# The second layer's mixer modulation computed inside the first layer's output projection instead of inside its GLA mixer

## The chip, the cores and the metric

The kernel is one inference step on one Trainium2 chip. It runs on one core. The metric is device time in microseconds (us) of one execution.

## What is computed

Two layers, each on 576 rows of width 1024 (512 prompt rows and 8 sequences of 8 sampled rows):

```
for l in range(DEPTH):
    mod = silu(c) @ w_ada[l] + b_ada[l]
    sh1, sc1, g1, sh2, sc2, g2 = split(mod, 6)
    h = x * (1.0 + sc1) + sh1
    mix, st = mixer(h, ...)
    x = layer_norm(ALPHA * x + g1 * mix)
    h = x * (1.0 + sc2) + sh2
    x = layer_norm(ALPHA * x + g2 * hier_moe(h, l, p))
```

The mixer projects `h` with `w_in` (1024 x 3096), runs three head groups (GLA linear attention, retention, Mamba-2 SSD), joins them and multiplies by `w_out` (1024 x 1024). `hier_moe` is a mixture of 16 experts. The modulation `mod` depends only on `c`, which is known from the start: nine rows (one prompt, eight samples) times `w_ada[l]`, 1024 x 6144, 24 MB in float32 for each layer. So it may be worked out at any time before it is used.

## The kernel before

**The modulation in groups and steps.** `ada_steps(l, g)` is a generator that works out a third of a layer's modulation: group 0 is sh1 and sc1, group 1 is g1 and sh2, group 2 is sc2 and g2. It has eight steps. A step loads 128 rows by 2048 columns of `w_ada` (1 MB, line 263) into a buffer `wada` and issues four matmuls of 32 x 512 (line 266), which add into one PSUM tile `ada`; the trace shows each as two rows, so a step is 8 rows there. After the eighth step comes a tail: line 269 adds the bias on DVE, which frees `ada`, and then for group 0 four transposes (line 300) and copies into `modT`, for group 1 a store to DRAM (line 272), for group 2 more work on DVE, four small loads and transposes (lines 279 to 292).

```
        for k in range(KD):
            w = wraw.tile([128, 2048], F32, name="wada", tag="raw")
            sp.dma_start(w, a["w_ada"][l, 128 * k:128 * (k + 1), c0:c0 + 2048])
            for q in range(4):
                ...
                pe.matmul(acc[32 * q:32 * q + 32, :], sc_[:, k, :], w[:, o:o + 512], start=(k == 0), stop=(k == KD - 1))
            yield
```

The buffer pool `wraw` has three buffers of 1 MB, and they are handed out in program order to everything that streams weights: `wada`, the pieces of `w_in` (line 382), the four pieces of `w_out` (line 1535), the first expert's weights (line 1288). All these loads are issued by SP's queue, in order: a load that waits for its buffer holds up what stands behind it.

**The stages of a layer.** `phase_a` runs SSD and then GLA, each woven with a piece of the input projection (lines 403 to 405) and, through `weave`, with modulation steps at a rate given by a table. The GLA mixer goes tile by tile (lines 808 to 965): its chain passes from PE through ACT, DVE and POOL and back. `phase_b` does the output projection in two passes over five row tiles (tile 4, of 64 rows, first). Pass 1 takes the SSD half of `w_out` (`load_out(2)`, `load_out(3)`), while the retention heads `ret` run beside it, two advances a tile; pass 2 takes `load_out(0)` and `load_out(1)`, the GLA and retention half, and after each tile a layer norm, the routing of tokens and the stores to `hbuf`. Each `w_out` piece is split into a high and a low part, in halves, by ACT (line 335) and DVE (line 336). A tile of a pass is 24 matmuls of 128 x 512 (lines 1564 to 1566), and its result is taken from PSUM by DVE (line 1576, `mix`, two a tile). `phase_b` also takes a generator `fill`: it is advanced three times after each tile of pass 1 and twice after each tile of pass 2. Then `experts` runs the mixture.

**Where the groups stand.** Group (0, 0) is computed at the start. A table says where the others go, as (layer, group): `MODS_SSD[l]` beside layer l's SSD, `MODS_GLA[l]` beside its GLA, `MODS_B[l]` in its output projection as `fill`. Before the change (1, 0) and (1, 1) stand in layer 0's GLA, and (1, 2) in layer 1's output projection. The program is scheduled when it is built: each engine gets one fixed order, and waits there in order.

Of the kernel before, what the change touches and what calls it, by code (L numbers as in the profile page):

```python
# [52 lines left out]
RORDER = (0, 4, 1, 2, 3)  # L53

MODS_SSD = (((0, 1), (0, 2),), ())
MODS_GLA = (((1, 0), (1, 1),), ())
MODS_B = ((), ((1, 2),))
MODS_RATE = ((1.5, 0.0), (1.7, 0.0))

C_GQ, C_GK, C_GV, C_GA, C_GR = 0, 128, 256, 512, 528  # L60
# [101 lines left out]
def _body(nc, tc, a, ctx, dbg):  # L162
# [1303 lines left out]
    def chain(*gens):  # L1466
        for g in gens:
            yield from g

    def phase_a(l, S, hT, gates, sL, z):  # L1470

        norms = []
        mods = [chain(*[ada_steps(*g) for g in w[l]]) for w in (MODS_SSD, MODS_GLA)]
        with ExitStack() as st:
# [721 lines left out]
    for l in range(L):  # L2196
        with ExitStack() as sL:
# [13 lines left out]
            with ExitStack() as rst:  # L2211
                fill = chain(*[ada_steps(*g) for g in MODS_B[l]])
                last, finish = phase_b(l, gates, nrm, gst, slots, rqk, rv, x, R, tabs, rst, fill)
# [123 lines left out]
```

## Time and profile before

| | |
|---|---|
| time, median of 3 runs | 1433.18 us (1431.92 to 1436.41) |
| the profiled execution, its own time | 1432.89 us |
| its span | 1431.1 us |
| PE busy | 1239.5 us, 87% of the span |
| weight loads of PE (PEld) busy | 940.2 us, 66% |
| DVE busy | 832.9 us, 58% |
| ACT, POOL busy | 487.9 us and 478.3 us |
| moved by DMA | 267.24 MB, mean 187 GB/s |

The span is the time from the first to the last instruction of the profiled execution. Busy shares are averages over stages that are bound by different things; a change in one stage is judged from that stage. The two layers run the same code, so a stage of layer 0 can be laid beside the same stage of layer 1, which differs in the modulation steps woven into it.

### The profile page before, as it was taken

Reading aid. Unit: us, or ns where it says so; the run is one execution under the profiler, and the core shown is the slowest. Engines: PE = TensorE matmul, PEld = TensorE weight load, DVE = VectorE, ACT = ScalarE, POOL = GpSimd, SP = SyncE. Lnnn points to the kernel's source line nnn. Section 1 sums busy time; section 2 is a strip of 40 time slices with the busy share of each in tenths; the row PEclk is TensorE's granted clock in tenths of the full one; section 3 lists DMA queues with packets and bytes.
Section 4 is the critical chain, followed back from the end, with each engine's and each line's share of the span. In section 5 each row is a group of like instructions: output and inputs, shape, how many; then the busy total and the mean of one; then the engine's idle time right before and its main releaser. Section 6 shows DMA issues by size and latency. Waiting matters only on the chain. (4 is left out here: it accounts for less than half of the span.)

```text
span 1431.1 us, 21969 instructions
## 1 busy us (share of the span) xinstructions
PE 1239.5 (87%) x8166; PEld 940.2 (66%) x8166; DVE 832.9 (58%) x1911; ACT 487.9 (34%) x902; POOL 478.3 (33%) x388
## 2 busy tenths in 40 slices
PE   4999999998986688989899998999998668998893
PEld 1998677775865356666479887877576446666661
DVE  0577457346889433446777647545598951324548
ACT  0552133331344213444355223333034431333422
POOL 0014112125244455541242312133413453534315
PEclk7899999999987699989999998999998779999997
DMA  9545665865162577987524410015555254887642
GB/s 317 177 148 167 224 231 190 303 217 178 38 195 101 173 283 283 395 306 237 177 89 148 120 60 30 23 41 193 196 183 183 99 201 199 320 319 261 214 142 107
DMA packets 100606, 267.24 MB, mean 187 GB/s; under 512 B 30871, under 2 KB 59449, under 8 KB 81528
## 3 DMA queue, kind: packets, MB, share of 16 engines
q1 hardware_dynamic: 84600, 246.62, 49.2%
q0 software_dynamic: 15872, 18.89, 4.0%
q8 instruction: 77, 1.26, 0.4%
q14 instruction: 57, 0.47, 0.1%
HBM read 246.84 MB, written 47.63 MB: 206 GB/s over the span
## 5 line engine op out<-in xcount | busy, mean ns | idle before, releaser
L403 PE MATMUL ps<-whi,hT 128*128 128x256 f32 (+1 forms) x640 | 188.4, 294 | 1.6 <-DVE yi L721 0.8
L405 PE MATMUL ps<-whi,hT 128*128 128x256 f32 (+1 forms) x640 | 182.9, 286 | 2.0 <-DVE rq L360 1.9
L404 PE MATMUL ps<-wlo,hT 128*128 128x256 f32 (+1 forms) x640 | 182.9, 286 | 1.1 <-DVE wlo L330 1.1
L403 PEld LDWEIGHTS ps<-whi,hT 128*128 128x128 f32 (+1 forms) x640 | 117.6, 184 | 14.7 <-issue 10.3
L404 PEld LDWEIGHTS ps<-wlo,hT 128*128 128x128 f32 (+1 forms) x640 | 117.4, 183 | 3.8 <-issue 2.1
L405 PEld LDWEIGHTS ps<-whi,hT 128*128 128x128 f32 (+1 forms) x640 | 117.2, 183 | 3.5 <-DVE rq L360 2.1
L1386 POOL DMA_INDIRECT ybuf<-ys,srci x36 | 46.9, 1302 | 132.5 <-issue 52.6
L330 DVE TENSOR_TENSOR wlo<-wraw,whi 128x2048 fp32r<-128x2048 f32 x30 | 68.6, 2287 | 34.5 <-ACT whi L329 34.1
L393 PE MATMUL ps<-hT,whi 128*128 128x288 f32 x512 | 88.5, 294 | 0.0
L330 DVE TENSOR_TENSOR wlo<-w3rd,whi 128x2048 fp32r<-128x2048 f32 x22 | 67.7, 3078 | 24.3 <-ACT whi L329 23.1
L1355 PE MATMUL ps<-whi,xh 128*128 128x256 f32 x384 | 59.8, 301 | 22.8 <-ACT xh L1342 12.7
L393 PEld LDWEIGHTS ps<-hT,whi 128*128 128x128 f32 x512 | 74.6, 188 | 0.4 <-ACT zdt L532 0.4
L1564 PE MATMUL ps<-whi,mh 128*128 128x512 f32 (+1 forms) x160 | 70.2, 439 | 3.7 <-ACT mh L1550 3.7
L266 PE MATMUL ada<-wada,scond 128*32 128x512 f32 x384 | 57.1, 667 | 17.4 <-DMA wada<-w_ada 17.4
L1566 PE MATMUL ps<-whi,ml 128*128 128x512 f32 (+1 forms) x160 | 68.2, 431 | 3.3 <-DVE ml L1551 3.3
L1355 PEld LDWEIGHTS ps<-whi,xh 128*128 128x128 f32 x384 | 52.5, 203 | 26.7 <-ACT xh L1342 13.6
L1565 PE MATMUL ps<-wlo,mh 128*128 128x512 f32 (+1 forms) x160 | 69.5, 434 | 0.0
L1355 PE MATMUL ps<-wlo,xh 128*128 128x256 f32 x384 | 59.8, 303 | 9.5 <-DVE wlo L330 9.4
L843 POOL TENSOR_TENSOR qh<-qx,ex 128x256 f32<-128x256 f32 x32 | 31.3, 1008 | 99.5 <-issue 82.1
L1355 PEld LDWEIGHTS ps<-wlo,xh 128*128 128x128 f32 x384 | 53.8, 208 | 12.4 <-DVE wlo L330 12.0
L329 ACT ACTIVATE whi<-wraw 128x2048 fp32r<-128x2048 f32 x30 | 57.3, 1910 | 12.5 <-PE ps L393 7.7
L1375 PE MATMUL ps<-w3rd,hid 128*128 128x512 f32 x128 | 58.6, 600 | 2.8 <-ACT hid L1366 2.8
(555 smaller groups left out, 2909.9 us busy)
## 6 DMA issues: line engine op xcount, KB each, us to landing
wada<-w_ada SPq DMA_DIRECT2D x48, 1024.0 KB
wraw<-moe_w SPq DMA_DIRECT2D x36, 1024.0 KB
slots<-moe_w SPq DMA_DIRECT2D x30, 1024.0 KB
w3rd<-moe_w SPq DMA_DIRECT2D x30, 1024.0 KB
wraw<-w_in SPq DMA_DIRECT2D x22, 1024.0 KB
wraw<-w_out SPq DMA_DIRECT2D x8, 1024.0 KB
ybuf<-bz SPq DMA_DIRECT2D x8, 512.0 KB
hbuf<-g SPq DMA_DIRECT2D x8, 512.0 KB
```

Of the source, the lines that this page charges most:

```text
L266: pe.matmul(acc[32 * q:32 * q + 32, :], sc_[:, k, :], w[:, o:o + 512], start=(k == 0), stop=(k == KD - 1))
L329: split.hi = act.activation(hi[:, :n], raw[:, :n], AF.Copy)
L330: dve.tensor_tensor(lo[:, :n], raw[:, :n], hi[:, :n].bitcast(F32), op=ALU.subtract)
L393: pe.matmul(p[:mw, :], lhs[:, k, m0:m0 + mw], rhs[:, k, 288 * h:288 * (h + 1)], start=(k == 0 and lhs is vh and rhs is hT[0]), stop=(k == ...
L403: pe.matmul(p[:n], hT[0][:, k, xs], vh[:, k, :], start=(k == 0), stop=False)
L404: pe.matmul(p[:n], hT[0][:, k, xs], vl[:, k, :], start=False, stop=False)
L405: pe.matmul(p[:n], hT[1][:, k, xs], vh[:, k, :], start=False, stop=(k == KD - 1))
L1355: pe.matmul(p, x[:, k], v[:, k], start=(x is self.xh and v is vh and k == 0), stop=(x is self.xl and k == KD - 1))
L1375: pe.matmul(p, self.hT[:, f], v[:, f, c], start=(f == 0), stop=(f == 1))
L1564: pe.matmul(p[:n], mh[:, k, :n], vh, start=(k == 0), stop=False)
L1565: pe.matmul(p[:n], mh[:, k, :n], vl, start=False, stop=False)
L1566: o = pe.matmul(p[:n], ml[:, k, :n], vh, start=False, stop=(k == 3))
```

## The change

Two entries of the table change. Groups (1, 0) and (1, 1) leave `MODS_GLA[0]` and enter `MODS_B[0]`: in layer 0's output projection `fill` now yields 16 steps and two tails, where it was empty. The rate table is not touched; in GLA there is nothing left for it to advance.

```diff
 MODS_SSD = (((0, 1), (0, 2),), ())
-MODS_GLA = (((1, 0), (1, 1),), ())
-MODS_B = ((), ((1, 2),))
+MODS_GLA = ((), ())
+MODS_B = (((1, 0), (1, 1)), ((1, 2),))
 MODS_RATE = ((1.5, 0.0), (1.7, 0.0))
```

Layer 1's order is the same on PE, DVE and ACT. In layer 0 the order changes from the end of SSD to the end of the output projection.

On PE in layer 0's GLA, ahead of the fourth tile's scores (the difference of the two orders, `-` before, `+` after; L266 is a modulation step of four matmuls each, L300 the tail of group 0, L858 and L861 the scores):

```order
 L404 MATMUL ps<-wlo,hT_190 128x256
 L405 MATMUL ps<-whi,hT_191 128x256
-L300 MATMUL ps<-cst,adas 128x128 x4
-L266 MATMUL ada<-wada,scond 32x512 x8
 L858 MATMUL ps<-qh,kh 64x256
 L861 MATMUL ps<-qh,kh 32x128 x2
```

All but one of the 16 steps leave the GLA in this way; the first one stays at its end, where the scheduler hoists it.

On PE in layer 0, from the last tile of pass 1 to the first of pass 2, after the change (L1564 to L1566 the projection, L1780 a small sum for the routing, L1546 the transposes of the gated heads):

```order
L1564 MATMUL ps<-whi,mh 128x512
L1565 MATMUL ps<-wlo,mh 128x512
L1566 MATMUL ps<-whi,ml 128x512
L266 MATMUL ada<-wada,scond 32x512 x12
L1780 MATMUL ps<-wm,cst 128x40 x8
L1546 MATMUL ps<-cst,gate_180 128x64 x2
L1546 MATMUL ps<-cst,gate_181 128x64 x2
L1546 MATMUL ps<-cst,gate_180 128x128 x2
L1546 MATMUL ps<-cst,gate_181 128x128 x2
```

Before, L1780 followed the projection directly. The three steps 13 to 15 stand here now; steps 2 and 3 stand at the first tile, 4 to 6, 7 to 9 and 10 to 12 in the next three tiles, and step 16 after pass 2's first tile.

On SP in layer 0's output projection, after the change (wada are steps 8 to 16, `w_out` x2 the two pieces for pass 2, brow the bias of group (1, 1), rope a table for the last retention tile):

```order
L1105 DMA ret_s<-slots 128x1024
L263 DMA wada<-w_ada 128x2048 x3
L260 DMA brow<-b_ada 32x512 x4
L263 DMA wada<-w_ada 128x2048 x5
L1023 DMA slots<-rope 128x2x256
L319 DMA slots<-ln 128x1024
L1535 DMA wraw<-w_out 128x2x1024 x2
L263 DMA wada<-w_ada 128x2048
L1288 DMA wraw<-moe_w 128x2048 x2
```

Before, all four pieces of `w_out` stood ahead of the third rope table of this stage, and nothing of `w_ada` stood in the stage.

## Rows read from the trace of the kernel before

**Rows 1.** Busy time per engine in matching stretches, layer 0 then layer 1.

```profile
core 0: us, PE busy (x) PEld busy (x) DVE busy (x) ACT busy (x) POOL busy (x), PEclk, DMA share, GB/s
225.25:303.20 77.95, 75.76 (x635) 54.41 (x633) 36.52 (x88) 25.05 (x69) 21.51 (x22) 1.00 0.67 237
303.20:331.87 28.67, 25.86 (x211) 22.41 (x212) 15.43 (x28) 11.05 (x21) 6.12 (x5) 1.00 0.63 209
331.87:399.83 67.96, 61.70 (x359) 44.10 (x360) 52.64 (x160) 14.98 (x31) 22.15 (x29) 0.95 0.37 118
399.83:478.75 78.92, 55.52 (x306) 44.22 (x306) 71.53 (x324) 32.98 (x52) 32.29 (x15) 0.75 0.37 125
897.75:970.55 72.80, 64.92 (x516) 55.34 (x515) 31.84 (x73) 24.50 (x67) 22.61 (x22) 0.93 0.11 35
970.55:999.21 28.66, 27.73 (x227) 22.78 (x228) 15.37 (x28) 11.06 (x21) 5.83 (x5) 1.00 0.61 207
999.21:1076.53 77.32, 70.43 (x407) 47.56 (x408) 56.16 (x165) 14.86 (x31) 23.62 (x29) 0.91 0.57 192
1076.53:1155.00 78.47, 55.23 (x308) 44.15 (x306) 71.92 (x324) 32.95 (x52) 32.15 (x15) 0.77 0.37 122
```

**Rows 2.** The same view for line 266 alone: PE and PEld busy.

```profile
225.25:303.20 77.95, 17.25 (x128) 3.04 (x128) 1.00 0.67 237
897.75:970.55 72.80, 2.10 (x8) 0.29 (x8) 0.93 0.11 35
999.21:1076.53 77.32, 4.71 (x40) 1.09 (x40) 0.91 0.57 192
```

**Rows 3.** Waits of PE in layer 1's GLA, 897.75 to 970.55.

```profile
PE ps L893 <- ACT PT L888: 3.2, 1, 3.2
PE ps L858 <- DVE kh L844: 1.6, 1, 1.6
```

**Rows 4.** Busy time in stretches of 2 us, layer 1's GLA.

```profile
908.00:910.00 2.00, 0.61 (x6) 0.41 (x4) 2.00 (x10) 0.38 (x1) 0.00 (x0) 1.00 0.00 0
910.00:912.00 2.00, 0.18 (x2) 0.18 (x2) 0.44 (x3) 1.23 (x4) 0.00 (x0) 1.00 0.00 0
914.00:916.00 2.00, 2.00 (x9) 1.82 (x8) 1.03 (x2) 0.60 (x1) 1.09 (x2) 0.50 0.00 0
```

**Rows 5.** Timeline of DVE, second `mix` of tiles; pass 1 then pass 2's first.

```profile
361.19 0.69 DVE L1576 TENSOR_TENSOR mix<-ps,g 128x512 f32<-128x512 f32 x1 [0.22 <-PE ps L1566]
370.16 0.69 DVE L1576 TENSOR_TENSOR mix<-ps,g 128x512 f32<-128x512 f32 x1
...
389.25 0.68 DVE L1576 TENSOR_TENSOR mix<-ps,g 128x512 f32<-128x512 f32 x1
...
399.83 0.68 DVE L1576 TENSOR_TENSOR mix<-ps,g 64x512 f32<-64x512 f32 x1 [2.36 <-PE ps L1566]
...
1029.73 0.69 DVE L1576 TENSOR_TENSOR mix<-ps,g 128x512 f32<-128x512 f32 x1 [1.74 <-PE ps L1566]
...
1041.67 0.69 DVE L1576 TENSOR_TENSOR mix<-ps,g 128x512 f32<-128x512 f32 x1
```

**Rows 6.** Timeline of PE: three steps, a tail, the first tile's start in layer 0.

```profile
1029.63 2.78 PE L266 MATMUL ada<-wada,scond 128*32 128x512 f32 x24
...
267.37 0.60 PE L300 MATMUL ps<-cst,adas 128*128 128x128 f32 x4
...
331.87 0.45 PE L1564 MATMUL ps<-whi,mh 128*64 128x512 f32 x1 [2.15 <-ACT mh L1550]
```

**Rows 7.** Timeline of PE in layer 1: two steps, then the first tile's start.

```profile
996.99 1.92 PE L266 MATMUL ada<-wada,scond 128*32 128x512 f32 x16
999.21 0.45 PE L1564 MATMUL ps<-whi,mh 128*64 128x512 f32 x1 [0.29 <-ACT mh L1550]
```

**Rows 8.** Issues of SP (timeline, then waits of SP in layer 1) and the first load's landing.

```profile
309.88 0.95 SPq L1535 DMA_DIRECT2D wraw<-w_out  x2
...
328.92 0.60 SPq L1535 DMA_DIRECT2D wraw<-w_out  x1
...
SPq L1535 <- PE ada L266: 6.8, 1, 6.8
...
3.53 18.23 SPq L263 DMA_DIRECT2D wada<-w_ada  x8
...
8.51 1.94 PE L266 MATMUL ada<-wada,scond 128*32 128x512 f32 x8 [8.51 <-DMA wada<-w_ada]
```

**Rows 9.** The split of `w_out`, all pieces: min/median/max in ns (ACT, then DVE).

```profile
L335 ACT ACTIVATE whi<-wraw,nrm x16: 1132/1142/1152, 312.0 to 1065.3; 128x1024 fp32r<-128x1024 f32 x16
L336 DVE SCALAR_TENSOR_TENSOR wlo<-wraw,nrm,whi x16: 1276/1284/1754, 313.2 to 1069.1; 128x1024 fp32r<-128x1024 f32 x16
```

## The prediction

> **What bounds the kernel now.** I start from the page: PE is the busiest engine (87% in the table above), so work moved on PE matters only where PE has, or hasn't, room. The page's average doesn't say where that is. The second view is the busy time of each engine in the stretches that the change touches, and since both layers run the same code, each stretch has a twin [rows 1]. The reader is to see three things. In layer 0's GLA (225.25 to 303.20) PE is busy for 75.76 of 77.95 us at full clock: it is full. In its twin in layer 1, with one modulation step instead of 16, PE is busy for 64.92 of 72.80 at a mean clock of 0.93: not full, and partly at half speed. In the output projection's pass 1, layer 0 takes 67.96 with no step, layer 1 takes 77.32 with five steps inside the stretch. The stretches between (28.67 and 28.66) and behind (78.92 and 78.47) are alike. So the twin stretches are a natural trial of both halves of the change: layer 1's GLA shows layer 0's GLA without the steps, and layer 1's pass 1 shows what steps cost there.
>
> The third view is line 266 alone [rows 2]: 128 rows and 17.25 us of PE in layer 0's GLA, 8 rows and 2.10 in layer 1's, 40 rows (five steps) in layer 1's pass 1. The fourth is the waits, and the fifth the timeline of the places where something ends or starts.
>
> **What it removes: the GLA.** 15 of 16 steps leave, 17.25 - 2.10 = 15.15 us of busy PE. The twin says what that is worth: 77.95 - 72.80 = 5.15 us. The other 10 go to two things. PE now waits for the mixer's own chain, 3.2 us for ACT's copies and 1.6 for DVE in the twin [rows 3]. And behind the idle stretch it runs slowly: with PE busy for 0.61 and 0.18 of two stretches of 2 us, the clock a little later stands at 0.50, the 1.2 GHz level [rows 4]. A mean of 0.93 over 72.80 us means that 72.80 x 0.07 = 5.1 us were lost to the clock, if PE had work throughout. So the gain is bounded by nothing from below (the order of the fillers differs a little from the twin's, and a wait could grow), by 5.15 + 5.1 = 10.2 if the clock never falls, and by 15.15 if nothing waits either. I take 6, near the twin's, since the chain and its waits are the same code; a little over it, since all that could differ is which wait falls at which moment, and the twin caught two falls of the clock.
>
> The page of the Trainium skill that bears on this speaks against the change: TensorE: Matmul & The Clock Gate (section What's actually happening) says that the slow clock is the default and activity releases it, so that taking filler matmuls out of a chain that waits costs clock as well. The trace agrees, with the 0.50 just named. By that rule the gain is 5.15; a gain of 10.2 is what it would be without the rule.
>
> **What it adds: the output projection.** Step by step, in layer 0:
> - Steps 2 and 3 stand ahead of the first tile. There PE waits 2.15 us for ACT's copy now [rows 6]; in layer 1 two steps of 1.92 fill the same place and 0.29 is left of the wait [rows 7]. Cost 0; if the wait were gone, 1.9.
> - Steps 4 to 12 are three steps in each of three tiles. Three steps run for 2.78 [rows 6]. Between second `mix` of neighbouring tiles layer 0 takes 370.16 - 361.19 = 8.97, layer 1 with three steps 1041.67 - 1029.73 = 11.94 [rows 5]: 2.97 for three, nothing hidden, because PE has no gap in these tiles. Nine steps cost 3 x 2.97 = 8.9.
> - The tail of (1, 0): four transposes, 0.60 on PE [rows 6]. Its work on DVE is hidden, since DVE is busy for 52.64 of 67.96 in pass 1 [rows 1]; without that cover the bias alone, a 128x512 operation like `mix`, would add 0.69 [rows 5].
> - Steps 13 to 15, and the loads behind them. The two pieces of `w_out` for pass 2 take the buffers of steps 13 and 14, so SP issues them only when these are done. Before, SP issues three pieces at 309.88 and 328.92 [rows 8], over 70 us ahead of pass 2's first `mix` at 399.83 [rows 5]. In layer 1 the second pair is held by a step too (6.8 us of SP's queue [rows 8]), but ahead of time. Now it is late by construction. From the end of pass 1's matmuls: 0.93 for step 13 (2.78 / 3), a load, which at the start of the program is 8.51 - 3.53 = 4.98 from issue to the first matmul [rows 8], four halves on ACT of 1.142 = 4.57, one half on DVE of 1.284 [rows 9]; the second load lands behind the first while ACT splits that. This makes 11.8, and about 0.5 for the last matmuls: 12.3 where now 399.83 - 389.25 = 10.6 lie between the two `mix` [rows 5]. So +1.7, and steps 14 and 15 are hidden in that wait. Bounds: 0, if the load is as quick as ACT is slow, and 4.6, if all four halves start only behind the second load.
> - Step 16 in pass 2: 0.93. The tail of (1, 1) is one DVE operation and a store.
> - What is queued behind. On SP the rope table of the last retention tile stands behind five `wada` that wait for buffers, and the first expert's weights behind all; both have a tile or more of time. On ACT the four splits now stand ahead of the last retention tile's copies, so that this head comes late by up to their 4.57. DVE waits at that moment anyway, and the head is needed three tiles later; I take 1 of 0 to 4.6.
> - The clock. Pass 1 has 0.95 in layer 0 and 0.91 in layer 1 [rows 1]: 67.96 x 0.05 = 3.4 and 77.32 x 0.09 = 7.0 lost. Steps there do not keep the clock up in the twin. I take 1 of 0 to 3.6.
>
> The load's 4.98 is a row. The Trainium skill (DMA: Bandwidth & Descriptors, section Anatomy of one DMA) fits a DMA of the GpSimd path by 2.0 us and bytes over 436 GB/s, which for 1 MB makes 4.4, an estimate; by it the term would be 1.1 instead of 1.7. The row, from SP's queue, decides.
>
> Sum: 8.9 + 0.6 + 1.7 + 0.9 + 1 + 1 = 14.1, less 6: **8 slower**. The profiled execution took 1432.89 by its own time, with a span of 1431.1; the median of the runs is 1433.18, 0.3 above. So 1433 + 8 = **1441**. All behind the projection is only shifted.
>
> **The rivals.** A difference below 0.3% (4.3 us) can't be told from no change.
> - *The GLA keeps its clock.* The fillers fall otherwise than in layer 1, PE never idles for long, and the gain is 10.2. For it: layer 0 runs at 1.00 now. Against: it does so with 15 steps as fillers, and the twin's waits of 3.2 and 1.6 come from ACT and DVE, which keep their work. Then 14.1 - 10.2 = +4: 1437, on the edge, and with the cheaper terms within 0.3%.
> - *Faster.* One mechanism: the GLA is a PE-bound stage (75.76 of 77.95), and all 15.15 come off, as if the chain had slack. It decides for faster only where the gain exceeds the cost by 4.3, so with a cost of 10.9 or less (8.9 + 0.6 + 0.9, all waits free: 10.4): 1433 + 10.4 - 15.2 = 1428. Against it the twin, which has the slack neither in PE nor in the chain.
> - *Each step costs more than its matmuls.* Layer 1's whole pass 1 is 77.32 - 67.96 = 9.36 longer with five steps, 1.87 a step, by waits, a heavier tail and clock. Twelve steps at that price are 22.4, with step 16 23.3, less 6: +17, 1450. For it: the whole row; against: the tile intervals, where a step costs 0.99, and group 2's tail, which isn't in this change.
> - That the change doesn't do what it says is excluded by the order shown above.
>
> **How the numbers follow.** The forecast 0.60, with its own range 1437 to 1445 (GLA 4 to 8, the three soft terms 1.5 to 6). The clock kept 0.19, faster 0.06, dear steps 0.15. Slower by over 0.3%: the forecast but for its lowest part, the dear steps, and the upper third of the clock kept: 0.76. Same 0.18, faster 0.06. The range from 1435 to 1448 leaves out the faster case and the upper half of the dear steps, under 0.15.
>
> **What would show it.** In the profile after: GLA of layer 0 from its first sum over `la` (line 808) to line 943 near 72, with a stretch at clock 0.50; PE waiting for ACT or DVE there. Tile intervals of pass 1 near 11.9 with line 266 three steps each; between the last `mix` of pass 1 and the first of pass 2 about 12.3, with ACT waiting for the DMA of `w_out`. Layer 1's stretches unchanged. I am wrong if GLA gains over 10 or pass 1's tiles stay near 9, which would mean that PE had gaps that I don't see; or if SP's queue holds something that I take for early.

## The result, and the profile after

The change makes the kernel slower: 1448.06 us (median of six) against 1431.59, a ratio of 1.0127 with a 95% interval of 1.0093 to 1.016. Timed again beside the experiments it took 1446.39, a ratio of 1.0088 (1.0059 to 1.0118). So the loss is 13.5 to 16.5 us where 8 were forecast; the sign was right, the size was not.

The profiled execution took 1456.35, the slowest of the six (span 1454.6). The rows show its busy time in the stretches of [rows 1]: the four of layer 0 (the GLA; the bridge, as this text calls the stretch from line 943 to the projection's first matmul; pass 1; pass 2), then two of layer 1.

```profile
227.40:294.50 67.10, 60.58 (x512) 51.96 (x510) 34.78 (x81) 24.27 (x67) 22.61 (x22) 0.97 0.15 51
294.50:325.30 30.80, 29.67 (x221) 24.32 (x221) 13.43 (x26) 10.83 (x21) 3.18 (x2) 0.94 0.52 182
325.30:410.30 85.00, 76.21 (x456) 47.14 (x457) 58.48 (x167) 14.18 (x30) 22.71 (x32) 0.94 0.68 249
410.30:494.10 83.80, 58.49 (x326) 45.83 (x324) 73.64 (x326) 34.24 (x56) 31.52 (x15) 0.79 0.44 145
...
921.00:993.70 72.70, 64.91 (x516) 55.06 (x515) 32.02 (x73) 24.51 (x67) 22.61 (x22) 0.93 0.11 35
...
1022.40:1099.70 77.30, 70.43 (x407) 47.61 (x408) 56.11 (x165) 14.81 (x31) 23.55 (x29) 0.91 0.55 192
```

Against [rows 1]: the GLA gains 10.9 and the bridge behind it loses 2.1, pass 1 loses 17.0, pass 2 4.9; in all 266.7 for 253.5, 13.2 slower. Layer 1's stretches are within 0.1 of theirs. This stage holds the loss; the rest of this execution's distance (the experts behind took 426.9) isn't in the second execution, where the same stretches take 68.1, 29.3, 86.6, 83.9 and the experts 418.8 against 419.0 before.

Inside pass 1 the timeline of DVE shows the `mix` of each tile, as in [rows 5] (the first tile's second `mix`, the second tile's two in one row, the second of each later tile, then pass 2's first).

```profile
334.26 0.67 DVE L1576 TENSOR_TENSOR mix<-ps,g 64x512 f32<-64x512 f32 x1
358.64 1.27 DVE L1576 TENSOR_TENSOR mix<-ps,g 128x512 f32<-128x512 f32 x2
...
370.35 0.68 DVE L1576 TENSOR_TENSOR mix<-ps,g 128x512 f32<-128x512 f32 x1
...
383.53 0.68 DVE L1576 TENSOR_TENSOR mix<-ps,g 128x512 f32<-128x512 f32 x1
...
396.17 0.69 DVE L1576 TENSOR_TENSOR mix<-ps,g 128x512 f32<-128x512 f32 x1
410.25 0.68 DVE L1576 TENSOR_TENSOR mix<-ps,g 64x512 f32<-64x512 f32 x1 [1.85 <-PE ps L1566]
```

The second tile's second `mix` starts near 359.2, so the intervals are 25.0, 11.1, 13.2, 12.6 and 14.1. The three tiles with three steps each take 36.9 where 389.25 - 361.19 = 28.06 stood [rows 5]: 8.9 for nine steps, as forecast. Two places were not: the first interval, 25.0 where the kernel before has 361.19 - 341.92 = 19.27 (the first of these in its rows below), and the switch between the passes, 14.1 for 10.6.

**The first interval.** Timelines of SP, POOL and PE around it, after:

```profile
318.03 2.31 SPq L315 DMA_DIRECT2D g<-mrow  x4
...
325.11 1.50 SPq L1023 DMA_DIRECT2D slots<-rope  x1
...
322.06 3.02 POOL L982 TENSOR_TENSOR gate<-gate,o 128x1280 f32<-128x1280 f32 x1 [27.81 <-DVE o L981]
...
331.10 0.73 POOL L1028 TENSOR_TENSOR slots<-qk,slots 64x256 f32<-64x256 f32 x1 [2.60 <-DMA slots<-rope]
...
336.26 0.69 PE L1036 MATMUL ps<-cst,slots 64*128 64x64 f32 x4 [2.79 <-DVE slots L1032]
...
339.11 2.99 PE L1085 MATMUL ps<-slots 128*32 128x64 f32 x30
```

and in the kernel before:

```profile
327.02 0.61 SPq L1023 DMA_DIRECT2D slots<-rope  x1
...
329.58 2.56 SPq L315 DMA_DIRECT2D g<-mrow  x4
...
330.59 1.50 POOL L1028 TENSOR_TENSOR slots<-qk,slots 64x256 f32<-64x256 f32 x1 [1.65 <-DMA slots<-rope]
...
341.92 0.68 DVE L1576 TENSOR_TENSOR mix<-ps,g 64x512 f32<-64x512 f32 x1
...
344.31 1.67 PE L1085 MATMUL ps<-slots 128*32 128x64 f32 x30
...
393.68 0.38 ACT L1037 ACTIVATE slots<-ps 128x256 f32<-128x256 f32 x1 [1.19 <-PE ps L1036]
```

The first retention tile needs a rope table. In the changed kernel SP issues it as POOL's gate (line 982) ends, at 325.1. Before, it went ahead of `g`, and POOL used it 3.6 us after the issue, 1.3 ahead of the projection's first matmul (331.87). After, the loads of `g`, `wr`, `br`, `iota` and `wm` stand ahead of it and three `wada` behind it; POOL used it 6.0 us after the issue, 5.8 behind the first matmul (325.3). PE waits 2.8 us for that head, and then 30 of its matmuls take 2.99 us instead of 1.67. The granted clock (the last but two of the figures) falls behind that wait. Busy time in the first tile, up to its second `mix`, and in the first interval, after and then before:

```profile
325.30:334.26 8.96, 6.99 (x30) 3.23 (x30) 6.85 (x12) 0.45 (x1) 4.63 (x7) 1.00 1.03 334
334.26:359.24 24.98, 21.81 (x141) 12.73 (x144) 14.00 (x39) 1.68 (x5) 10.42 (x15) 0.86 0.31 112
```

```profile
331.87:341.92 10.05, 8.62 (x25) 4.40 (x26) 7.61 (x15) 0.44 (x1) 4.62 (x6) 0.66 0.89 280
341.92:361.19 19.27, 16.58 (x122) 10.15 (x123) 11.49 (x32) 1.68 (x5) 8.75 (x12) 1.00 0.32 98
```

Before, the clock's loss lies in the first tile (10.05 x 0.34 = 3.4). After, the first tile keeps the 2.4 GHz level and the interval behind the wait loses 24.98 x 0.14 = 3.5, over half of the 5.7 by which it grew.

**The switch.** Timelines of SP, ACT and PE at the end of pass 1, after:

```profile
396.59 1.24 SPq L1535 DMA_DIRECT2D wraw<-w_out  x2
...
400.92 1.05 ACT L2001 ACTIVATE slots<-slots 128x1024 f32<-128x1024 f32 x1
401.87 0.59 ACT L1550 ACTIVATE mh<-ps 128x512 fp32r<-128x512 f32 x1
402.35 4.26 ACT L335 ACTIVATE whi<-wraw,nrm 128x1024 fp32r<-128x1024 f32 x4
412.89 0.38 ACT L1037 ACTIVATE slots<-ps 128x256 f32<-128x256 f32 x1 [6.29 <-PE ps L1036]
...
403.55 0.68 PE L1564 MATMUL ps<-whi,mh 128*64 128x512 f32 x2 [2.42 <-ACT whi L335]
```

`w_out` is late as forecast, but ACT's four halves start 5.8 us after the issue, behind two other copies, and all four then run in a row. The last retention head (line 1037) is copied at 412.89, 2.6 behind pass 2's first `mix`; before, at 393.68 (last row of the rows of before), it was 6.2 ahead of it. At that moment ACT is not held by the splits: it has waited 6.29 us for PE's line 1036.

### The profile page after: what moved, and what is told of

Its sections match the earlier page's. It is cut to its first block, busy times and chain, and to the rows that moved or that the text cites. A ratio compares the mean times of both kernels' runs of the same rounds, so it can differ in the third digit from the quotient of the medians.

```text
span 1454.6 us, 21960 instructions
## 1 busy us (share of the span) xinstructions
PE 1253.6 (86%) x8166; PEld 949.0 (65%) x8166; DVE 838.2 (58%) x1911; ACT 487.3 (34%) x902; POOL 473.7 (33%) x388
## 5 line engine op out<-in xcount | busy, mean ns | idle before, releaser
L403 PEld LDWEIGHTS ps<-whi,hT 128*128 128x128 f32 (+1 forms) x640 | 119.2, 186 | 16.1 <-issue 10.3
L405 PEld LDWEIGHTS ps<-whi,hT 128*128 128x128 f32 (+1 forms) x640 | 118.7, 186 | 2.8 <-DVE hT L495 2.5
L1355 PE MATMUL ps<-whi,xh 128*128 128x256 f32 x384 | 59.2, 299 | 22.9 <-ACT xh L1342 12.7
L266 PE MATMUL ada<-wada,scond 128*32 128x512 f32 x384 | 57.7, 670 | 18.8 <-DMA wada<-w_ada 18.8
L1564 PE MATMUL ps<-whi,mh 128*128 128x512 f32 (+1 forms) x160 | 70.4, 442 | 3.6 <-ACT whi L335 2.4
L1566 PE MATMUL ps<-whi,ml 128*128 128x512 f32 (+1 forms) x160 | 67.7, 427 | 2.6 <-DVE ml L1551 2.6
L843 POOL TENSOR_TENSOR qh<-qx,ex 128x256 f32<-128x256 f32 x32 | 32.2, 1037 | 88.0 <-issue 69.2
L329 ACT ACTIVATE whi<-wraw 128x2048 fp32r<-128x2048 f32 x30 | 57.3, 1910 | 10.6 <-PE ps L393 7.7
```

The lines of the kernel that those rows point to most:

```text
L329: split.hi = act.activation(hi[:, :n], raw[:, :n], AF.Copy)
L403: pe.matmul(p[:n], hT[0][:, k, xs], vh[:, k, :], start=(k == 0), stop=False)
L405: pe.matmul(p[:n], hT[1][:, k, xs], vh[:, k, :], start=False, stop=(k == KD - 1))
L1355: pe.matmul(p, x[:, k], v[:, k], start=(x is self.xh and v is vh and k == 0), stop=(x is self.xl and k == KD - 1))
L1564: pe.matmul(p[:n], mh[:, k, :n], vh, start=(k == 0), stop=False)
L1566: o = pe.matmul(p[:n], ml[:, k, :n], vh, start=False, stop=(k == 3))
```

## The experiments

Each kernel's stage in layer 0 (line 808 to 943, to line 1564, pass 1, pass 2), read as in [rows 1] from one profiled execution, and its time over five rounds. Line numbers of an edited kernel are shifted by a few.

| kernel | GLA | bridge | pass 1 | pass 2 | sum | median | ratio to before (95%) |
|---|---|---|---|---|---|---|---|
| before | 78.0 | 28.7 | 68.0 | 78.9 | 253.5 | 1431.6 to 1432.9 | 1 |
| changed, again | 68.1 | 29.3 | 86.6 | 83.9 | 267.9 | 1446.39 | 1.0088 (1.0059 to 1.0118) |
| none | 64.5 | 30.8 | 74.5 | 78.4 | 248.2 | 1439.98 | 1.004 (1.002 to 1.0061) |
| mmonly | 65.1 | 30.7 | 68.7 | 79.0 | 243.5 | 1489.95 | 1.0379 (1.0337 to 1.0421) |
| pass2 | 68.0 | 30.8 | 76.8 | 103.6 | 279.2 | 1475.85 | 1.0276 (1.0244 to 1.0309) |
| early | 67.9 | 28.0 | 79.4 | 85.5 | 260.8 | 1444.82 | 1.007 (1.0044 to 1.0095) |
| late | 77.6 | 29.2 | 68.4 | 79.2 | 254.4 | 1432.37 | 0.9987 (0.9965 to 1.0008) |
| nolast | 67.1 | 29.3 | 82.2 | 88.0 | 266.6 | 1447.0 | 1.0098 (1.0074 to 1.0123) |
| half | 71.6 | 28.9 | 72.0 | 79.6 | 252.1 | 1427.25 | 0.995 (0.9931 to 0.9968) |
| ropefirst | 68.2 | 29.4 | 82.5 | 85.4 | 265.5 | 1444.93 | 1.0103 (1.0071 to 1.0135) |
| keep4 | 65.0 | 29.9 | 81.6 | 78.9 | 255.4 | 1435.84 | 1.0019 (0.9991 to 1.0048) |
| early4 | 65.1 | 28.0 | 75.5 | 78.1 | 246.7 | 1426.84 | 0.9971 (0.9946 to 0.9995) |
| keep12 | 75.2 | 30.8 | 67.3 | 78.5 | 251.8 | 1429.53 | 1.0004 (0.9969 to 1.0039) |

The sums carry the argument, since the stretches outside the stage vary by several us between executions of the same code (the start 223.5 to 229.6, layer 1's GLA 70.0 to 74.5). Each sum is one execution; the changed kernel's two have 266.7 and 267.9, so a difference of one or two us between sums says little.

**after2**, the changed kernel unedited.

> The changed kernel again, unedited, beside the three below on the same chip. The trace shown with the result is of the slowest of its six executions (1456.35, median 1448.06); 8 of its 23 us come behind the stage that was changed. Theory A (the whole loss of about 16 lies between line 808 and line 1427 of layer 0): a more usual execution has a span near 1446, layer 0 from line 808 to the first sum of the experts (line 1427) takes 266 to 268 where it took 253.5, and behind it the 419 of before. Theory B (the stage only starts it; the experts behind it are slower as well, by the clock or by late loads): those 419 are 423 or more again.

Theory A holds: 267.9 in the stage, 418.8 in the experts.

**none**, no steps at all.

```
+        if l == 1 and g < 2:
+            dve.memset(acc, 0.0)
...
+            if l == 1 and g < 2:
+                yield
+                continue
             w = wraw.tile([128, 2048], F32, name="wada", tag="raw")
```

> Leaves out the loads and matmuls of the groups (1, 0) and (1, 1) altogether (the sums are set to zero, so layer 1 is modulated by the bias alone). What is left is the gain of the GLA without the price of the steps. Theory A (late chain): GLA and the stretch behind it take the 98 of the changed kernel, about 9 less than before, but the first tile's retention follows POOL's gate and not PE, so some 7.5 of it arrive; pass 1 and pass 2 are as before (68, 79): about 1424, 7 to 9 below the kernel before, and 23 to 25 below the changed one, which is then the price of 16 steps, 1.5 a step. Rival (the gain was over-read, the clock takes it back): pass 1 without steps runs at a lower clock, over 70, and the kernel is only 3 to 6 below before; the steps' price is then 20 or so. As forecast before the result, the gain would be 6 and the price 14.

The rival's pass 1: without a single step it takes 74.5, and of the GLA's gain only 5.3 are left in the sum. Rows of the GLA and of pass 1:

```profile
226.20:290.70 64.50, 58.07 (x504) 50.56 (x502) 36.72 (x84) 24.44 (x69) 21.60 (x22) 1.00 0.19 63
...
321.50:396.00 74.50, 64.45 (x363) 46.67 (x364) 55.52 (x167) 15.23 (x33) 23.84 (x32) 0.91 0.30 97
```

PE is idle for 10.0 us of pass 1 (6.3 before) and the clock is 0.91. Its median says nothing of the change: layer 1, modulated otherwise, sends its tokens to other experts, and their stretch takes 289.6 for 276. So part of pass 1's loss isn't the steps' at all, and the question became what starts late there.

**mmonly**, the matmuls without their loads (`alone` is layer 1's groups 0 and 1; the loads are skipped for them).

```
-                pe.matmul(acc[...], sc_[:, k, :], w[:, o:o + 512], ...)
+                pe.matmul(acc[...], sc_[:, k, :], bc(ident, 1, 4) if alone else w[:, o:o + 512], ...)
```

> The matmuls of the 16 steps stay, and everything behind them, but they read the identity that lies in SBUF (layer 1 is modulated by other numbers); their 16 loads of 1 MB are gone, and so w_out for pass 2 is loaded early again. Theory A (late chain): without loads the interval between pass 1's last mix and pass 2's first goes back to about 10.6 plus three steps at most (13.4), and pass 2 no longer waits for a late retention head: 4 to 7 us faster than the changed kernel. Rival (the steps cost what PE spends in them, the loads are free): within 2 us of the changed kernel. Second rival (the loads also slow the other transfers and engines in pass 1): over 8 us faster.

The time is spoilt by the experts (339.7 in layer 1, which is modulated by other numbers). The stage speaks for the second rival, and beyond it. Line 266's share (line 270 there) in the GLA, the bridge and pass 1:

```profile
227.30:292.40 65.10, 5.76 (x46) 1.24 (x46) 1.00 0.14 47
292.40:323.10 30.70, 4.83 (x26) 0.93 (x26) 1.00 0.49 169
323.10:391.80 68.70, 6.22 (x47) 1.04 (x46) 1.00 0.32 104
```

Their 16.8 us of matmuls are there, more than half of them drawn ahead into the GLA and the bridge, and the stage takes 243.5, 10 less than before and 5 less than with no steps. So without loads and buffers the matmuls cost the stage nothing; but they also stand elsewhere (only 17 of these 119 rows fall in the three tiles where the changed kernel has three steps each), and the run doesn't part the two.

**pass2**, all steps in pass 2: `range(0 if l == 0 else 3)` in pass 1's loop, `range(4 if l == 0 else 2)` in pass 2's.

> The same 16 steps, none in pass 1, four behind each tile of pass 2 of layer 0. In pass 2 before, PE is busy for 55.5 of 78.9 us and waits for DVE and ACT, and both pieces of w_out are loaded ahead of the steps. Theory A (the price comes from a stage in which PE has no gap, and from w_out behind the steps' buffers): pass 1 takes 68 again, the switch 10.6, and of the 15 us of PE in pass 2 at least half lie in gaps: pass 2 grows by 0 to 7, so 1424 to 1432 in all, no slower than the kernel before. Rival (each step costs its PE time wherever it stands in the projection): pass 2 grows by 14 to 17, about 1440. Second rival (the steps' loads hold back the experts' first weights): pass 2 ends early, but the first sums of the experts wait for a load, and the time is over 1440.

The second rival, in another place. Waits of PE in pass 2, then SP's issues:

```profile
PE ps L1419 <- DMA qk<-hbuf,srci: 13.2, 1, 13.2
```

```profile
460.41 18.07 SPq L263 DMA_DIRECT2D wada<-w_ada  x4
478.57 0.86 SPq L1640 DMA_DIRECT2D hbuf<-g  x2
...
493.97 0.58 SPq L1640 DMA_DIRECT2D hbuf<-h2p  x1
```

Four `wada` that wait for buffers hold SP's queue for 18 us, the stores of the normalized tiles stand behind them, and PE waits 13.2 us for the experts' gather, which reads what they store. My reading that pass 2 had gaps on PE was right, and worth nothing.

**early**, the GLA's end ahead of the remaining pieces.

```
+                    with tc.issue_after(gla.ends[0].ins), tc.issue_after(gla.ends[1].ins):
+                        weave((), fill, mods[1])
...
+            with tc.issue_after(gla.ends[1].ins):
+                ws = [load_out(2), load_out(3)]
```

> The changed kernel with one thing put back: in layer 0 the end of the GLA (the eight matmuls of line 950, the square sqt of line 975 and what hangs on it) is queued ahead of the remaining projection pieces and of w_out's splits, so that the square starts 9 to 12 us behind line 943 instead of 17.6 to 19.1, and POOL's gate (line 982) near 19 instead of 26. Theory A (the gain of the GLA is given back because the retention's first tile waits for this chain): the steps stay where they are, and pass 1 is 5 to 8 us shorter, 77 to 81 instead of 85 to 86.6; about 1440. Rival (pass 1 is longer for the steps and the clock alone): pass 1 stays over 84 and the time within 2 us of the changed kernel.

The stage gains as theory A has it: pass 1 79.4, the first interval 18.5, the sum 7 less than the changed kernel. The median falls by only 1.6, with runs from 1430.8 to 1449.5, so the time alone doesn't show it. In early the rope table too is issued sooner (3.9 ahead of the first matmul, 0.2 in the changed kernel), so late and ropefirst take the norm and the table apart.

**late**, the mirror image in the kernel before: two more `next(fill)` ahead of the norm, and the norm under `issue_after` of the last `tanh`.

> The mirror image: the kernel before, all 16 steps in the GLA, with one thing made worse. In layer 0 the square sqt of line 975 is queued on ACT behind two more pieces' copies, so that it starts some 18 us behind line 943 instead of 12.9, and POOL's gate near 26 instead of 20.8. Theory A (a late norm delays the retention, and pass 1 pays): GLA unchanged at 77.9, the bridge at 28.7, pass 1 is 72 to 75 instead of 67.9 without a step in it: 4 to 7 slower than before, 1437 to 1440. Rival (the norm has slack up to the retention, and what the stripped kernel lost in its pass 1 came from the clock behind a less busy GLA): pass 1 within 1.5 of 67.9, the time the same as before.

Theory A falls. The norm is late (POOL's gate 25.5 behind line 943), and almost nothing follows. Timelines of POOL and DVE:

```profile
326.59 3.01 POOL L982 TENSOR_TENSOR gate<-gate,o 128x1280 f32<-128x1280 f32 x1 [26.20 <-DVE o L981]
...
333.35 0.72 POOL L1028 TENSOR_TENSOR slots<-qk,slots 64x256 f32<-64x256 f32 x1 [0.74 <-DMA slots<-rope]
...
339.74 0.67 DVE L1584 TENSOR_TENSOR mix<-ps,g 64x512 f32<-64x512 f32 x1
...
360.11 0.69 DVE L1584 TENSOR_TENSOR mix<-ps,g 128x512 f32<-128x512 f32 x1 [0.23 <-PE ps L1574]
```

The rope table, issued at 329.63, was used 3.7 us later, 3.1 behind the first matmul (330.3), and the interval is 20.4. So a late norm alone isn't enough; the table has to be slow as well.

**ropefirst**, the changed kernel with that table alone moved ahead of `g`.

```
+            behind = tc.issue_after(sp.dma_start(rope0[0], a["rope"][:, :, ORDER[0]]).ins)
+        with behind:
+            load_mod_rows(g1, l, 0, 0)
...
```

> The changed kernel, with one thing moved in SP's queue: in layer 0 the load of the first rope table stands ahead of the loads of g, wr and br, no longer behind them. The norm at the end of the GLA stays late (POOL's gate some 26 us behind line 943). Theory C (the rope table lands late because, issued behind POOL's gate, it finds the four g loads, wr, iota, wm and three wada on the DMA engines): POOL's first rope product (line 1028) starts 3 to 4 us behind the first matmul of line 1564 instead of 5.8, the first tile's interval is 21 to 23 instead of 25, and pass 1 is 2 to 4 us shorter, less what the first mix now waits for g. Rival (the late norm is all): first interval still 24 to 25.6, pass 1 over 84.

Theory C. Timelines of SP, POOL and DVE:

```profile
324.61 0.61 SPq L1518 DMA_DIRECT2D slots<-rope  x1
...
327.97 0.73 POOL L1032 TENSOR_TENSOR slots<-qk,slots 64x256 f32<-64x256 f32 x1
...
334.86 0.68 DVE L1587 TENSOR_TENSOR mix<-ps,g 64x512 f32<-64x512 f32 x1
353.06 1.27 DVE L1587 TENSOR_TENSOR mix<-ps,g 128x512 f32<-128x512 f32 x2
```

With the norm as late as ever the first product starts 3.1 behind the first matmul and the interval is 18.8, 6.8 less than the changed kernel's 25.6 beside it. Pass 1 keeps 4.1 of that: the first `mix` waits for `g`, and the three `wada` behind it come 4.6 us later (the next interval is 13.1 for 11.1). Pass 2 takes 1.5 more, so the sum gains 2.4, and the time isn't better than the changed kernel's. The forecast of theory C held, its reason isn't shown: the move puts `g`, `wr` and `br` behind the table and the `wada` later at once, and in late, where those loads stand ahead as in the changed kernel, the table takes 3.7 and not 6.0. All kernels together make a scale, of POOL's first rope product against the projection's first matmul:

| product behind the matmul by | first interval | clock in it |
|---|---|---|
| -1.6 (half), -1.3 (before), -0.9 (keep12), -0.5 (early4), -0.1 (early) | 18.1, 19.3, 18.6, 19.1, 18.5 | 1.00 in all |
| 3.1 (ropefirst), 3.1 (late), 3.4 (mmonly) | 18.8, 20.4, 21.4 | 1.00 in all |
| 4.3 (pass2), 4.8 (none), 4.8 (keep4) | 23.4, 23.4, 25.1 | 0.93, 0.93, 0.86 |
| 5.2 (nolast), 5.8 and 5.8 (changed) | 24.1, 25.0 and 25.6 | 0.93, 0.86 and 0.87 |

Up to 3.1 us the interval is at most 20.4; from 4.3 on it is 23.4 or more and the clock falls in it, with steps in pass 1 or without.

**nolast**, `range(3 if l == 1 or i + 1 < NT else 0)` in pass 1's loop.

> The changed kernel without the three steps behind the last tile of pass 1; they go to pass 2, two behind each tile, and so both pieces of w_out for pass 2 are loaded ahead of them. Theory A (late w_out costs 3.5 at the switch): from pass 1's last mix to pass 2's first 10.6 to 11.1 instead of 14 to 15, pass 1 some 3 to 4 us shorter, pass 2 up to 3 longer by the three steps: 0 to 3 faster than the changed kernel. Rival (steps in pass 2 hold the stores of the normalized tiles in SP's queue): pass 2 grows by 4 or more, and the kernel is slower than the changed one.

Neither alone. The switch falls to 12.7 and pass 1 by 4.4, but pass 2, with three steps in it (24 rows of line 266), grows by 4.1: the sum is 1.3 less, the time the same.

**keep4**, four steps left in the GLA, so none behind `w_out`: one generator feeds both places, the GLA through `islice(shared[0], 4)` at a rate of 0.45.

> Four of the 16 steps stay in layer 0's GLA (0.45 behind each of its parts), twelve go to the projection, three behind each of the first four tiles, so no step stands behind pass 1's last tile or in pass 2. The norm and the rope table stand as late as in the changed kernel. Theory A (w_out behind the last steps costs about 3.5 at the switch, and with the last retention head behind the splits 5 in pass 2): the stretch from line 808 to 1427 of layer 0 is 258 to 261 instead of 267, pass 2 back at 79 to 80: about 1438 to 1440. Rival (only the number of steps counts, some 1.2 us each net of what the GLA gains): 4 of 16 fewer give back a quarter of the loss, 263 to 264, 1443.

Better than theory A in the stage, 255.4, and in the time. Timeline of DVE at the switch, then busy time in pass 2:

```profile
393.37 0.68 DVE L1581 TENSOR_TENSOR mix<-ps,g 128x512 f32<-128x512 f32 x1
403.61 0.68 DVE L1581 TENSOR_TENSOR mix<-ps,g 64x512 f32<-64x512 f32 x1 [2.36 <-PE ps L1571]
```

```profile
403.60:482.50 78.90, 56.40 (x308) 44.90 (x306) 71.43 (x324) 32.94 (x53) 32.31 (x15) 0.74 0.36 126
```

The switch is 10.2 and pass 2 78.9: both losses go with the steps behind the last tile and in pass 2. The first interval stays at 25.1, with the rope table behind `g`.

**early4**, keep4 with early's edit.

> The same twelve steps in the projection and four in the GLA, and the end of the GLA (line 950's matmuls, the square sqt) queued ahead of the remaining projection pieces and w_out's splits, which also puts the rope table ahead of g in SP's queue. Nothing stands late in it but the steps themselves. Theory A: first interval 18 to 20, pass 1 74 to 76, pass 2 79 to 80, the stretch 250 to 254, at or below the kernel before: 1427 to 1433. Rival (twelve steps cost more than a full GLA gives back, however they are placed): the stretch over 257, 1437 or more.

Theory A, and past it. Its stage, as in [rows 1]:

```profile
228.40:293.50 65.10, 63.14 (x543) 51.64 (x542) 34.40 (x81) 24.60 (x67) 21.50 (x22) 1.00 0.34 118
293.50:321.50 28.00, 27.71 (x227) 22.90 (x227) 13.47 (x28) 10.93 (x21) 5.46 (x5) 1.00 0.59 203
321.50:397.00 75.50, 69.82 (x435) 45.22 (x436) 59.35 (x166) 15.36 (x33) 21.55 (x29) 1.00 0.72 253
397.00:475.10 78.10, 55.55 (x308) 44.12 (x306) 71.10 (x324) 32.91 (x53) 32.34 (x15) 0.75 0.39 127
```

With both late places mended the move pays: 246.7, 6.8 less than before, and 0.29% (0.05 to 0.54) in the time. It is keep4 with early's edit, which is worth 8.7 in the stage and 9.0 in the median there.

**half**, `MODS_GLA = (((1, 0),), ())`, `MODS_B = (((1, 1),), ((1, 2),))`, rate 0.9.

> Half of the change: the eight steps of (1, 0) stay in the GLA, at 0.9 behind each of its parts instead of 1.7, the eight of (1, 1) go to the projection (ahead of the first tile and behind the first three). The end of the GLA stands on the engines as in the kernel before. Theory A (the loss is the late norm, the late w_out and about 1 us a step in pass 1, not the move as such): GLA 70 to 73, pass 1 73 to 75 with six steps in its tiles, no late w_out, the switch near 10.6: about 1432 to 1436, within 0.3% of before. Rival (each step costs 1.5 to 1.9 in the projection wherever it comes from): eight steps cost 12 to 15, the GLA gives 5, so 1440 to 1443.

The stage is as theory A has it: the GLA gives 6.3, pass 1 takes 4.0. The time is below both kernels and below theory A, by 0.5% (0.3 to 0.7) of before; the stage shows only 1.4 of these 7 us, and where the rest comes from its one profile (of the slowest run, 1433.75) doesn't tell.

**keep12**, twelve steps left in the GLA.

> Twelve of the 16 steps stay in the GLA (1.3 behind each part), four go to the projection, ahead of the first tile and behind it. With 16 in the GLA the stretch from line 808 to 1427 took 253.5, with 8 it took 252.1 and the kernel was 0.5% faster. Theory A (the projection's free places, the wait ahead of the first tile above all, take the first steps for nothing, and the GLA is PE-bound over 8 to 16 steps): GLA 74 to 75, bridge 29, pass 1 68 to 70, 251 to 253: 1427 to 1431. Rival (the gain of the half was the clock's, and goes with the GLA full): 1432 to 1434.

The stage is as theory A has it, 251.8; the time can't be told from before.

## Why the prediction was wrong

- *What it removes: 6, "near the twin's".* Mis-sized: the GLA and the bridge together gain 8.7 and, in the second execution, 9.2. The stretch is 67.1, not near 72. The twin was one draw: layer 1's GLA alone takes 70.0 at a mean clock of 0.98 and 74.5 at 0.91 in executions of these kernels, and in the changed kernel's own two 72.7 at 0.93 and 70.2 at 0.98. The clock does fall, to 0.97 and 0.95, so the rival in which it keeps its clock isn't what happened. Yet the GLA alone gains 10.9 and 9.9, above and just below the 10.2 that the text gave for a clock that never falls, and its sign of being wrong, "if GLA gains over 10", came up in one of the two. So the twin was no bound: in it PE is busy for 64.92 us and idle for 7.9, here 60.58 and 6.5.
- *Steps 2 and 3: 0.* Right; the first tile's second `mix` even comes 1.1 sooner behind the first matmul (9.0 for 10.1).
- *Steps 4 to 12: 8.9, the tail 0.6.* Right in sum: 8.9 together, for 9.5. In early4, at a clock of 1.00 throughout pass 1, the same three tiles take 37.9, 9.8 more than before, so this cost is not the clock's.
- *What is queued behind.* This is the step that failed. It looked at the rope table of the last retention tile, and gave "a tile or more of time". The one that was late is the first, which has no term: it is issued when POOL's gate ends, the gate comes later against the projection's start than before (0.2 ahead of it where 4.9 stood), and the table then takes 6.0 from issue to use where 3.6 stood. That is 5.7 in the first interval; ropefirst gives 6.8 back by one move in SP's queue (2.4 of it stay in the sum), and keep4, in which the table stands as in the changed kernel, still has its 25.1. The text named this as what would make it wrong: "if SP's queue holds something that I take for early".
- *Steps 13 to 15: 1.7 of 0 to 4.6.* Mechanism right, size at the other end: 3.5, and 4.6 in the second execution. The sum let ACT begin when the load lands and split one piece under the second load. In the trace two copies stand ahead of the splits on ACT, and all four halves run behind them.
- *Step 16 (0.9) and the last retention head (1 of 0 to 4.6).* 4.9 together. Mis-sized, and the reason isn't shown. The argument "the head is needed three tiles later" let a head be late that then works beside the first normalizations, on DVE, which is busy for 73.6 of pass 2's 83.8. But neither the late head nor the late splits are needed for the loss. ACT copies the head 7.0 ahead of pass 2's first `mix` in early and 6.0 ahead in ropefirst (rows of ACT, early then ropefirst), and pass 2 takes 85.5 and 85.4 there. In nolast `w_out` is issued 24 us ahead of that `mix`, and pass 2 takes 88.0. What goes with the loss is a step in pass 2: all kernels with rows of line 266 there take 83.8 or more, all without 78.1 to 79.6. How a step of 1.06 us of PE comes to cost 5 stays open.

```profile
397.55 0.38 ACT L1037 ACTIVATE slots<-ps 128x256 f32<-128x256 f32 x1 [0.17 <-PE ps L1036]
...
401.40 0.39 ACT L1041 ACTIVATE slots<-ps 128x256 f32<-128x256 f32 x1 [0.85 <-PE ps L1040]
```

- *The clock: 1.* 85.0 x 0.06 = 5.1 lost in pass 1, where 3.4 were: 1.7, and 3.5 by the second execution's 0.92. It is no term beside the others, since the intervals hold it: 3.5 of it lie in the first interval (0.86) and 14.1 x 0.12 = 1.7 in the switch (0.88).
- *Sum.* By terms -8.7 - 1.1 + 5.7 + 8.9 + 3.5 + 4.9 = 13.2, the stage's loss. Of the rivals, the dear steps gave the right size (1450) for the wrong reason: they ask 1.87 a step in pass 1, where the three tiles show 0.99, and pass 1 grows by 7.5 in early4 with nine steps in it (72 rows of line 266) and by 4.0 in half with five (40 rows). Why layer 1's pass 1 is 9.4 longer with five wasn't looked into. Part of the misses cancel: the GLA and the bridge gave 2.7 more than forecast.

Layer 0's GLA ran at a clock of 1.00 in all seven kernels with four steps or more in it (before, late, half, keep12, keep4, early4, mmonly), and with fewer at 0.95 to 0.97 in six executions and at 1.00 in one (none). Four steps kept back (keep4, early4) make that stretch 2 to 3 us shorter than the changed kernel's, with more PE work in it. The Trainium skill (TensorE: Matmul & The Clock Gate, What's actually happening) says that activity releases the throttle; by that rule a GLA with fewer matmuls beside its chain can lose clock; six of these seven executions agree, and none, at 1.00, does not.

What stays open: why the medians of early and half differ from before by other amounts than their stages do, what a step in pass 2 holds up, and what exactly slows the rope table's load (below).

## What to carry to other kernels

When work with loads is moved, list every transfer that changes its place in the issuing queue and ask of each who is the first to wait for it; one table behind a freed buffer, late by a few us, made 5.7 here, of a loss of 13.2. Steps that hold the buffers of the next stage's weights belong ahead of the point from which those weights must be on their way, so move a part and stop there: here eight of the 16 steps, or twelve with the GLA's end queued ahead, not all. A stretch of the twin layer is one draw of a clock that varies; before it stands as a term, see how far the same code differs between executions.

## What was not expected of the hardware

The same rope table was used 3.4 us after its issue in ropefirst (DMA share 0.47 in that stretch), 3.6 before (0.55), and 6.0 in the changed kernel (1.03), but 3.7 in late with a share of 0.94, and 4.9 in none (1.08), which has no `wada` there at all: neither the share nor those loads alone explain it. And the same layer 1 GLA took from 70.0 to 74.5 us, in step with its mean granted clock from 0.98 to 0.91.
